# A two-layer attention trunk: buffers, load order and engine for the first unit of value weights

## The chip, the cores and the metric

The kernel runs on one core of a Trainium2 chip. The metric is the device time of one execution in microseconds, median of several. Engines are named as in the profile: PE is TensorE (matmuls), PEld its loading of the stationary operand, DVE VectorE, ACT ScalarE, POOL GpSimd, and SP the engine whose queue issues the DMA transfers.

## The reference

The trunk has two layers. Each takes the RMS norm of the running state h, runs a token mixer with a gate, projects the result and adds its norm to h. Layer 0 mixes by dilated window attention in three groups of 16 heads, layer 1 by differential attention. x has 1024 tokens of 1024 channels, all in float32.

```python
for i in range(DEPTH):                      # 2
    u = rmsnorm(h, norm_pre[i])
    y = dilated_mixer(u, ...) if i % 2 == 0 else diff_mixer(u, ...)
    h = h + rmsnorm(y, norm_post[i])

def dilated_mixer(h, w_in, w_out):
    proj = h @ w_in                         # q, k, v of 3 x 16 heads, and the gate
    ...                                     # v: 3 x 1024 columns
    y = o.reshape(B, S, DIL_WIDTH) * jax.nn.silu(gate)
    return y @ w_out
```

What this case is about is the very first part: the norm of x, its transposition, and the first 512 of the 3072 value columns of layer 0.

## The kernel before, in words

A float32 matmul is done as three matmuls with operands split in a high and a low part: `high` is a cast to a reduced type, `low` is what the cast left out (full minus high). So each weight piece passes three steps: a load into a tile `raw`, a cast on ScalarE into the high tile (`split`, L184), and a subtraction into the low tile (`low`, L122), on the engine that is handed in. The split state of x, transposed, stays in two large tiles, `XH` and `XL`.

The value columns of layer 0 come in six units (`values0(g, u)`), each 1024 x 512 weights. `v_weights` brings a unit in four pieces of 128 x 1024 floats (512 KB): two make one pair of tiles `vwh`, `vwl`, of which three pairs exist. Piece by piece, its tile `raw` comes from `raw_tile`, a ring of two buffers shared by all weights of the kernel. Then, for each of eight blocks of 128 tokens, `v_block` gives 24 matmuls (L213: eight k tiles, and for each high x high, high x low, low x high); the result is copied and split into `vs` (L513 on ScalarE, L122 on VectorE) and stored to DRAM (L515).

The first unit is woven into the start: blocks of x are loaded (L522), normed (`normed`: square and sum on ScalarE, a power on GpSimd, L135, one multiplication on VectorE, L144, that yields `xn`), and transposed on TensorE in eight small matmuls (`to_xt`, L153); ScalarE copies the result to XH (L158), VectorE writes XL. After the transposes of a block come the 24 matmuls of that block, then the next block. The generator of the unit is advanced twice behind the load of block 0 of x, which writes the loading and splitting of its four pieces at that place of the program. The start pool lies on the right side of the on-chip memory and is closed after the first unit.

The order on TensorE is the order of the program. On the other engines, SP's queue among them, a scheduler orders the instructions when the kernel is built: in the order of the program as far as their inputs and buffers are there by its estimated times; otherwise a later instruction goes ahead. A queue then runs strictly in that order, and each instruction waits on the chip for what it needs. The second unit (`values0(0, 1)`) follows in the program after the start.

Of the kernel before, what the change touches and what calls it, by code (L numbers as in the profile page):

```python
# [10 lines left out]
F32 = mybir.dt.float32  # L11
# [7 lines left out]
P = 128  # L19
T = 1024  # L20
D = 1024
# [71 lines left out]
def trunk(ctx: ExitStack, tc: tile.TileContext, a: dict, out: bass.AP):  # L93
    nc = tc.nc
# [26 lines left out]
    def low(eng, o, full, hi):  # L121
        eng.tensor_tensor(o, full, hi.bitcast(F32), ALU.subtract)  # L122
# [15 lines left out]
    def normed(pool, rows, g_b, bufs=None):  # L138

        ss = pool.tile([P, 1], F32, tag="ss", name="ss")  # L140
        xn = pool.tile([P, D], F32, tag="xn", name="xn", bufs=bufs)
        nc.scalar.activation(xn, rows, AF.Square, accum_out=ss)
        r = rstd(pool, ss, 1.0 / D, "pre")
        nc.vector.scalar_tensor_tensor(xn, rows, r, g_b, ALU.mult, ALU.mult)  # L144
        return xn

    def to_xt(xn, n, tag):

        for c in range(2):
            pt = ps.tile([P, 512], F32, tag=tag, name="pt_x")  # L150
            for j in range(4):
                kt = 4 * c + j
                nc.tensor.transpose(  # L153
                    out=pt[:, ts(j)], in_=xn[:, ts(kt)], identity=ident
                )
            src = pt.rearrange("p (j q) -> p j q", j=4)
            hi = XH[:, 4 * c : 4 * c + 4, ts(n)]
            nc.scalar.copy(hi, src)  # L158
            low(nc.vector, XL[:, 4 * c : 4 * c + 4, ts(n)], src, hi)
# [5 lines left out]
    def ts(j, w=P):  # L165
        return slice(j * w, (j + 1) * w)

    def bcast_row(pool, src, tag):
        t = pool.tile([P, D], F32, tag=tag, name=tag, bufs=1)
        nc.sync.dma_start(t, src.partition_broadcast(P))  # L170
        return t


    def raw_tile(shape):
        return wp.tile(shape, F32, tag="raw", name="raw", bufs=2)
# [7 lines left out]
    def split(wh, wl, raw, eng=None):  # L183
        nc.scalar.copy(wh, raw)  # L184
        low(eng or alt(), wl, raw, wh)

    def load(w, shape):
        raw = raw_tile(shape)
        nc.sync.dma_start(raw, w)
        return raw  # L190


    def v_weights(pool, tags, w, n, step, eng):

        parts = []
        for c in range(0, KT, 4):
            wh, wl = (pool.tile([P, 4, n], F32R, tag=t, name=t) for t in tags)
            for k in range(0, 4, step):
                split(wh[:, k : k + step], wl[:, k : k + step],
                      load(w[:, c + k : c + k + step, :], [P, step, n]), eng)  # L200
            parts.append((wh, wl))
            yield 0
        yield parts

    def v_block(parts, n, b, o, first, last):

        k = 0
        for c in range(2):
            for j in range(4):
                wh, wl = (t[:, j, :] for t in parts[c])  # L210
                xh, xl = (t[:, 4 * c + j, ts(b)] for t in (XH, XL))
                for l, r_ in ((xh, wh), (xh, wl), (xl, wh)):
                    nc.tensor.matmul(o, lhsT=l, rhs=r_, start=first and k == 0,  # L213
                                     stop=last and k == 3 * KT - 1, skip_group_check=True)
                    k += 1
                    yield n
# [3 lines left out]
    def qk_unit(pool, unit, w, sub=1, on_pool=False):  # L220

        tiles = []
        for half in range(2):
            wh, wl = w_tiles([P, KT, P])
            split(wh, wl, load(w[half], [P, KT, P]))
            tiles.append((wh, wl))
# [51 lines left out]
    def gate_units(pool, layer, w, fs, eng=None, prepare=None):  # L278

        for f in fs:  # L280
            wh, wl = w_tiles([P, KT, P])
            split(wh, wl, load(w[f], [P, KT, P]), eng)
            if prepare and f == fs[-1]:
                prepare()
                banks = [ps.tile([P, 512], F32, tag="pj", name="pg") for _ in range(2)]
                for k0 in (0, EARLY):
                    for c in range(2):
                        yield from project(banks[c], wh, wl, ts(c, 512), range(k0, k0 + EARLY))
                for c in range(2):
                    yield f, c, banks[c]  # L290
                return
            for c in range(2):
                o = ps.tile([P, 512], F32, tag="pj", name="pg")
                yield from project(o, wh, wl, ts(c, 512))
                yield f, c, o

    def gates(pool, layer, w, fs):

        for v in gate_units(pool, layer, w, fs, nc.vector):
            if type(v) is tuple:  # L300
                f, c, o = v
                s = pool.tile([P, 512], F32, tag="sil", name="sil", bufs=2)
                nc.scalar.activation(s, o, AF.Silu)
                nc.sync.dma_start(sil_d[layer][f, :, ts(c, 512)], s)
                written.add(("gate", layer, f))
            else:
                yield v
# [15 lines left out]
    def run(gen):  # L323
        for _ in gen:
            pass
# [175 lines left out]

    with tc.tile_pool(name="v0", bufs=3) as vp:

        def values0(g, u, eng=nc.vector):
            for parts in v_weights(vp, ("vwh", "vwl"), a["dil_v"][g, u], 512, 2, eng):
                if parts == 0:
                    yield 0
            for b in range(NB):
                pv = ps.tile([P, 512], F32, tag="pj", name="pv")
                yield from v_block(parts, 512, b, pv, True, True)  # L510
                vs = vp.tile([P, 8, 2, HD], F32R, tag="v", name="vs")
                src = pv.rearrange("p (h f) -> p h f", h=8)
                nc.scalar.copy(vs[:, :, 0, :], src)  # L513
                low(nc.vector, vs[:, :, 1, :], src, vs[:, :, 0, :])
                nc.sync.dma_start(  # L515
                    v0_d[g, ts(b), 8 * u : 8 * u + 8, :], vs.rearrange("p h e f -> p h (e f)").bitcast(F32))

        with tc.tile_pool(name="start", bufs=2, side="right") as sp:
            blocks, g_b, v = [], None, values0(0, 0, nc.gpsimd)
            for n in range(NB):  # L520
                xb = sp.tile([P, D], F32, tag="xb", name="xb", bufs=6)
                nc.sync.dma_start(xb, x_v[n])  # L522
                blocks.append(xb)
                if n == 0:
                    g_b = bcast_row(sp, a["norm_pre"][0], "g_b")
                    next(v)
                    next(v)
            for n in range(NB):
                to_xt(normed(sp, blocks[n], g_b), n, "pt")
                for _ in range(24):  # L530
                    next(v)
            run(v)
        run(values0(0, 1))
        run(gates(vp, 0, a["dil_g"], range(8 - LATE0)))
        for g in (1, 2):
            for u in range(2):
                run(values0(g, u))
# [11 lines left out]
    with tc.tile_pool(name="l0", bufs=2) as lp:  # L549
# [216 lines left out]
        for i in range(nst + LAG_P):  # L766
            if i < nst:
                hd, c = heads[i // 4], i % 4
# [16 lines left out]
            if 0 <= i - LAG_T < nst:  # L785
                hd, c = heads[(i - LAG_T) // 4], (i - LAG_T) % 4
# [4 lines left out]
            if 0 <= i - LAG_P < nst:  # L791
                hd, c = heads[(i - LAG_P) // 4], (i - LAG_P) % 4
# [7 lines left out]
    with tc.tile_pool(name="o0", bufs=2, reuse_waits="tile") as op:  # L800
# [10 lines left out]
        def values1(pool, v2, **kw):  # L811

            for parts in v_weights(wp, ("wh", "wl"), a["diff_v"][v2], 256, 4, nc.vector):
                if parts == 0:
                    yield 0
            for b2 in range(NB // 2):
                pv = ps.tile([P, 512], F32, tag="pj", name="pv")


                for e in range(2):  # L820
                    yield from v_block(parts, 256, 2 * b2 + e, pv[:, ts(e, 256)], e == 0, e == 1)
                vs = pool.tile([P, 2, 2, 2, P], F32R, name="vs", **kw)
                src = pv.rearrange("p (b h f) -> p (b h) f", b=2, h=2)
                hi = vs.rearrange("p b h e f -> p (b h) e f")
                nc.scalar.copy(hi[:, :, 0, :], src)
                low(nc.vector, hi[:, :, 1, :], src, hi[:, :, 0, :])
                for e in range(2):
                    nc.sync.dma_start(
                        v1_d[2 * v2 : 2 * v2 + 2, 2 * b2 + e].rearrange("h k c -> k h c"),
                        vs[:, e].rearrange("p h e f -> p h (e f)").bitcast(F32),  # L830
                    )
            written.add(("v", v2))


        v = values1(op, 0, tag="pq")
# [43 lines left out]
    with tc.tile_pool(name="l1", bufs=2) as lp:  # L879
# [163 lines left out]
        for hd in heads:  # L1043
# [7 lines left out]
            for c in range(4):  # L1051
                start, n = h + LAG + c * (c + 1) / 20, c + 1
# [50 lines left out]
```

## Time and profile before

| | |
|---|---|
| time, median of 3 runs | 2029.63 us (2026.72 to 2030.63) |
| the profiled execution | 2031.38 us, its span 2029.5 us |
| mean granted TensorE clock | 0.981 |
| busy: PE, PEld, DVE, ACT, POOL | 94%, 79%, 56%, 44%, 30% of the span |
| DMA | 397.90 MB, mean 196 GB/s |

Times in the profile are microseconds from the start of the span. A row of the timeline gives the start, the duration, the engine, the line of the kernel and what is written from what; in square brackets is how long the engine stood idle before, and who released it. A row of the chain gives start, duration and the engine or transfer that the chain passes through. A row by stretches gives the stretch, its length and the busy time (with the count of instructions) of PE, PEld, DVE, ACT and POOL, then the granted clock of TensorE, the busy share of the DMA engines and GB/s.

### The profile page before, as it was taken

Reading aid. Unit: us, or ns where it says so; the run is one execution under the profiler, and the core shown is the slowest. Engines: PE = TensorE matmul, PEld = TensorE weight load, DVE = VectorE, ACT = ScalarE, POOL = GpSimd, SP = SyncE. Lnnn points to the kernel's source line nnn. Section 1 sums busy time; section 2 is a strip of 40 time slices with the busy share of each in tenths; the row PEclk is TensorE's granted clock in tenths of the full one; section 3 lists DMA queues with packets and bytes.
Section 4 is the critical chain, followed back from the end, with each engine's and each line's share of the span. In section 5 each row is a group of like instructions: output and inputs, shape, how many; then the busy total and the mean of one; then the engine's idle time right before and its main releaser. Section 6 shows DMA issues by size and latency. Waiting matters only on the chain.

```text
span 2029.5 us, 28888 instructions
## 1 busy us (share of the span) xinstructions
PE 1905.9 (94%) x10008; PEld 1594.5 (79%) x10008; DVE 1143.0 (56%) x2771; ACT 888.0 (44%) x2057; POOL 618.0 (30%) x386
## 2 busy tenths in 40 slices
PE   6999999999999998989898978899999999999898
PEld 4788888888878787878787867788878788887776
DVE  3312122146676768676768674571057877878626
ACT  3312122125555555555555565352244445545632
POOL 2000000043353535353535340040471533524111
PEclk8999999999999999999999989999999999999999
DMA  5424244377696969697878889553356555555753
GB/s 208 146 88 140 87 156 152 113 221 229 191 300 195 291 202 293 195 282 218 267 234 240 256 284 294 162 176 107 129 174 193 175 176 164 169 196 182 274 160 125
DMA packets 218018, 397.90 MB, mean 196 GB/s; under 512 B 40976, under 2 KB 123408, under 8 KB 217872
## 3 DMA queue, kind: packets, MB, share of 16 engines
q1 hardware_dynamic: 217872, 396.04, 61.3%
q8 instruction: 80, 1.31, 0.3%
q14 instruction: 66, 0.54, 0.1%
HBM read 254.87 MB, written 132.71 MB: 191 GB/s over the span
## 4 chain that ended last, share of the span: by engine, by line
PE 62%; DMA 13%; DVE 12%; ACT 4%; POOL 4%; issue 3%; SPq 1%; POOLq 0%; DVEq 0%; ACTq 0%
PE pqk L274 22%; PE pv L213 16%; PE pg L274 8%; PE po L386 4%; PE sc L921 2%; PE pe L439 2%; PE up L646 2%; PE sc L596 2%; DMA wb<-wt_d 2%; PE ob L974 2%; DMA st_d<-st 2%; PE tp L619 2%; DVE u L669 1%; POOL r L252 1%; DVE pm L924 1%
## 5 line engine op out<-in xcount | busy, mean ns | idle before, releaser
L274 PE MATMUL pqk<-XL,wh 128*128 128x512 f32 x1024 | 421.1, 411 | 0.0
L274 PE MATMUL pqk<-XH,wh 128*128 128x512 f32 x1024 | 409.3, 400 | 1.7 <-DVE t L251 1.7
L274 PE MATMUL pqk<-XH,wl 128*128 128x512 f32 x1024 | 410.5, 401 | 0.0
L606 ACT ACTIVATE pm<-pm,st 128x128 f32<-128x128 f32 (+1 forms) x384 | 170.2, 444 | 159.7 <-DVE st L603 158.1
L122 POOL TENSOR_TENSOR wl<-raw,wh 128x1024 fp32r<-128x1024 f32 x35 | 84.0, 2400 | 500.6 <-ACT wh L184 500.6
L274 PEld LDWEIGHTS pqk<-XH,wh 128*128 128x128 f32 x1024 | 194.3, 190 | 30.6 <-DVE t L251 2.4
L274 PEld LDWEIGHTS pqk<-XL,wh 128*128 128x128 f32 x1024 | 194.4, 190 | 27.5
L274 PEld LDWEIGHTS pqk<-XH,wl 128*128 128x128 f32 x1024 | 194.8, 190 | 27.0
L250 POOL TENSOR_TENSOR r<-t 128x512 f32<-128x512 f32 x64 | 98.2, 1535 | 266.7 <-DVE t L249 265.7
L122 DVE TENSOR_TENSOR wl<-raw,wh 128x1024 fp32r<-128x1024 f32 x61 | 82.0, 1345 | 149.1 <-ACT wh L184 148.6
L213 PE MATMUL pv<-vwh,XH 128*128 128x512 f32 x384 | 155.8, 406 | 7.0 <-ACT XH L158 4.0
L184 ACT CAST wh<-raw 128x1024 fp32r<-128x1024 f32 x96 | 100.5, 1047 | 140.3 <-PE pqk L274 61.8
L213 PE MATMUL pv<-vwl,XH 128*128 128x512 f32 x384 | 154.9, 403 | 2.8 <-POOL vwl L122 2.8
L213 PE MATMUL pv<-vwh,XL 128*128 128x512 f32 x384 | 154.8, 403 | 0.9 <-DVE XL L122 0.3
L122 DVE TENSOR_TENSOR vs<-pv,vs 128x512 fp32r<-128x512 f32 x64 | 44.2, 691 | 197.3 <-ACT vs L513 191.3
L931 ACT ACTIVATE pm<-pm,mx 128x256 f32<-128x256 f32 (+7 forms) x128 | 99.4, 776 | 120.3 <-DVE mx L930 61.8
L122 DVE TENSOR_TENSOR pp<-tp,pp 128x512 fp32r<-128x512 f32 (+2 forms) x192 | 104.0, 542 | 73.6 <-ACT pp L623 72.0
L619 PE MATMUL tp<-ident,pm 128*128 128x128 f32 x560 | 95.7, 279 | 39.2 <-DVE pp L122 38.2
L603 DVE CUSTOM_DVE_ANT_0 pm<-sc,masks 128x128 f32<-128x128 f32 (+1 forms) x384 | 118.8, 344 | 20.8 <-PE sc L596 19.4
L619 PEld LDWEIGHTS tp<-ident,pm 128*128 128x128 f32 x560 | 72.6, 143 | 73.5 <-issue 34.2
L924 DVE CUSTOM_DVE_ANT_0 pm<-sc,md 128x512 f32<-128x512 f32 (+3 forms) x192 | 102.5, 551 | 32.9 <-PE sc L921 30.1
L513 ACT CAST vs<-pv 128x512 fp32r<-128x512 f32 x48 | 28.2, 587 | 189.9 <-PE pv L213 188.7
(514 smaller groups left out, 4483.6 us busy)
## 6 DMA issues: line engine op xcount, KB each, us to landing
qk_d<-rh SPq DMA_DIRECT2D x64, 512.0 KB
qk_d<-r SPq DMA_DIRECT2D x64, 512.0 KB
qh<-qk_d SPq DMA_DIRECT2D x128, 256.0 KB
ql<-qk_d SPq DMA_DIRECT2D x128, 256.0 KB
ka<-qk_d SPq DMA_DIRECT2D x64, 512.0 KB
v_d<-vs SPq DMA_DIRECT2D x48, 512.0 KB
raw<-in_dil_qk_dram SPq DMA_DIRECT2D x48, 512.0 KB
vt<-v_d SPq DMA_DIRECT2D x48, 512.0 KB
```

The source lines that it names most:

```text
L122: eng.tensor_tensor(o, full, hi.bitcast(F32), ALU.subtract)
L184: nc.scalar.copy(wh, raw)
L213: nc.tensor.matmul(o, lhsT=l, rhs=r_, start=first and k == 0, stop=last and k == 3 * KT - 1, skip_group_check=True)
L250: nc.gpsimd.tensor_sub(put(r[0]), nat(t1), nat(t2))
L274: nc.tensor.matmul(o, lhsT=l[:, kt, :], rhs=r_[:, kt, tok], start=kt == 0 and k == 0, stop=kt == KT - 1 and k == 2)
L386: nc.tensor.matmul(banks[c], lhsT=l[:, kt, ts(n)], rhs=r_[:, ts(c, 512)], start=first and k == 0, stop=last and k == 2,)
L439: nc.tensor.matmul(bank, lhsT=l[:, kt, ts(n)], rhs=r_[:, ts(c, 512)], start=kt == 0 and k == 0, stop=kt == EARLY - 1 and k == 2)
L603: nc.vector.tensor_tensor_reduce(pm[:, cols], sc[:, cols], m[:, m.shape[1] - w_ :], 1.0, 3.0e38, ALU.add, ALU.min, st[:, 0, j : j + 1])
L606: nc.scalar.activation(pm[:, cols], pm[:, cols], AF.Exp, bias=st[:, 0, j : j + 1], scale=-1.0, accum_out=st[:, 1, j : j + 1])
L619: nc.tensor.transpose(out=tp[:, ts(n)], in_=self.pb.pop((b, kb)), identity=ident)
L924: nc.vector.tensor_tensor_reduce(pm[:, k0:k1], sc[:, :w_], m_, 1.0, 3.0e38, ALU.add, ALU.min, mx[:, j : j + 1])
L931: nc.scalar.activation(pm[:, :wq], pm[:, :wq], AF.Exp, bias=mx[:, 0:1], scale=-1.0, accum_out=den)
```

## The change

The four pieces of the first unit no longer use the shared ring of two raw buffers but a ring of four in the start pool; the ring of x's blocks in the same pool goes from six buffers to four. The order of the program stays, but with a buffer free for each piece, no load of the unit has to wait for a buffer. The subtractions of the first unit go from GpSimd to VectorE, where those of the other units are. The shared ring of two is not used by the first unit any more.

```diff
-    def load(w, shape):
-        raw = raw_tile(shape)
+    def load(w, shape, raw=None):
+        raw = raw or raw_tile(shape)
         nc.sync.dma_start(raw, w)
         return raw
...
-    def v_weights(pool, tags, w, n, step, eng):
+    def v_weights(pool, tags, w, n, step, eng, raw=lambda: None):
...
                 split(wh[:, k : k + step], wl[:, k : k + step],
-                      load(w[:, c + k : c + k + step, :], [P, step, n]), eng)
+                      load(w[:, c + k : c + k + step, :], [P, step, n], raw()), eng)
...
-        def values0(g, u, eng=nc.vector):
-            for parts in v_weights(vp, ("vwh", "vwl"), a["dil_v"][g, u], 512, 2, eng):
+        def values0(g, u, **kw):
+            for parts in v_weights(vp, ("vwh", "vwl"), a["dil_v"][g, u], 512, 2, nc.vector, **kw):
...
-            blocks, g_b, v = [], None, values0(0, 0, nc.gpsimd)
+
+            blocks, g_b = [], None
+            v = values0(0, 0, raw=lambda: sp.tile([P, 2, 512], F32, tag="raw", name="raw", bufs=4))
             for n in range(NB):
-                xb = sp.tile([P, D], F32, tag="xb", name="xb", bufs=6)
+                xb = sp.tile([P, D], F32, tag="xb", name="xb", bufs=4)
```

## The prediction

> **What bounds the kernel now.** I read the page first, then the chain that ended last, cut to the first 35 us, then the timeline of SP's queue and of TensorE there, then busy time by stretches.
>
> ```profile
> span 2029.5 us, 28888 instructions
> PE 1905.9 (94%) x10008; PEld 1594.5 (79%) x10008; DVE 1143.0 (56%) x2771; ACT 888.0 (44%) x2057; POOL 618.0 (30%) x386
> 90.00:500.00 410.00, 410.00 (x1837) 332.79 (x1836) 110.79 (x184) 99.97 (x174) 46.54 (x25) 1.00 0.44 148
> 500.00:700.00 200.00, 188.05 (x1039) 158.83 (x1038) 144.10 (x377) 107.89 (x305) 86.05 (x49) 0.98 0.80 239
> ```
>
> The first figures of a stretch are its length and the busy time of PE; the last three are granted clock, DMA share and GB/s. PE is busy 94% of the span and without a gap from 90 to 500 us, so a microsecond by which its stream reaches 90 us earlier is carried on for at least 410 us; later there are gaps (12 us in 200). What the change touches lies ahead of 90 us. The chain there:
>
> ```profile
> 2.13 6.63 DMA raw<-in_dil_v_dram
> ...
> 8.78 1.05 ACT vwh L184
> ...
> 12.29 6.73 DMA raw<-in_dil_v_dram
> ...
> 19.05 1.05 ACT vwh L184
> ...
> 22.49 2.37 POOL vwl L122
> ...
> 24.88 3.60 DMA raw<-in_dil_v_dram
> ...
> 29.58 1.23 DVE vwl L122
> 30.81 0.60 DVE vs L122
> 31.41 0.61 DVE XL L122
> ...
> 32.06 7.77 PE pv L213 x22
> ```
>
> Until 32 us the chain is weights: a load, its cast on ScalarE, its subtraction on GpSimd, which frees the buffer for the next load; from then on it is matmuls. SP's queue says why the third load goes out only at 12.29:
>
> ```profile
> 2.13 0.91 SPq L189 DMA_DIRECT2D raw<-in_dil_v_dram  x2
> 3.08 2.90 SPq L522 DMA_DIRECT2D xb<-in_x_dram  x5
> 8.85 0.33 SPq L522 DMA_DIRECT2D xb<-in_x_dram  x1
> 12.29 2.66 SPq L189 DMA_DIRECT2D raw<-in_dil_v_dram  x2
> 16.49 0.33 SPq L522 DMA_DIRECT2D xb<-in_x_dram  x1
> ...
> 31.43 39.64 SPq L515 DMA_DIRECT2D v_d<-vs  x6
> ```
>
> There are two raw buffers, so pieces 2 and 3 of the first unit wait for GpSimd, and six blocks of x have gone ahead of them. On TensorE (start, length, idle before):
>
> ```profile
> 10.37 0.79 PE L213 MATMUL pv<-vwh,XH 128*128 128x512 f32 x1
> 12.32 0.80 PE L213 MATMUL pv<-vwl,XH 128*128 128x512 f32 x1 [1.16 <-POOL vwl L122]
> 16.76 0.42 PE L213 MATMUL pv<-vwh,XL 128*128 128x512 f32 x1
> 20.15 0.76 PE L213 MATMUL pv<-vwh,XH 128*128 128x512 f32 x1 [2.97 <-ACT vwh L184]
> 22.58 0.79 PE L213 MATMUL pv<-vwl,XH 128*128 128x512 f32 x1 [1.67 <-POOL vwl L122]
> 27.27 1.04 PE L153 MATMUL pt_x<-ident,xn 128*128 128x128 f32 x8
> 32.06 0.79 PE L213 MATMUL pv<-vwh,XL 128*128 128x512 f32 x1 [0.27 <-DVE XL L122]
> 37.32 0.40 PE L213 MATMUL pv<-vwh,XL 128*128 128x512 f32 x1
> 39.65 1.04 PE L153 MATMUL pt_x<-ident,xn 128*128 128x128 f32 x8
> 41.82 0.50 PE L213 MATMUL pv<-vwh,XL 128*128 128x512 f32 x1
> 47.05 1.04 PE L153 MATMUL pt_x<-ident,xn 128*128 128x128 f32 x8
> 26.00:27.00 1.00, 1.00 (x3) 0.72 (x3) 0.00 (x0) 0.99 (x1) 0.00 (x0) 0.50 0.52 184
> 27.00:27.50 0.50, 0.50 (x5) 0.39 (x4) 0.48 (x1) 0.00 (x0) 0.00 (x0) 0.96 0.98 393
> 34.00:37.00 3.00, 3.00 (x9) 2.32 (x8) 0.67 (x1) 0.00 (x0) 0.00 (x0) 0.50 0.46 183
> ```
>
> Block 0 has 24 matmuls, from 10.37 to the transposes at 27.27. It loses 1.16 + 2.97 + 1.67 = 5.80 us waiting for weights, and all of it runs slow: from 32.06 to 37.32 there are 12 steps of 0.43 to 0.44 us from one matmul to the next, with a granted clock of 0.50 in the rows of 34 to 37 and 26 to 27, and block 0 has the same step (eleven matmuls from 12.32 to 16.76; I take 0.425); from 41.82 to 47.05 there are 22 of 0.238 us. So block 1 (27.27 to 39.65, 12.38 us) is dear too: block 2 takes 7.40.
>
> **The change part by part.** *Buffers and loads.* The four pieces of the first unit get four buffers of their own in the start pool; x's fall from six to four. With no wait left, the four loads stand in program order behind the first x block and the row of norm weights, and ahead of x's blocks 1 to 3. The two shared raw buffers are free from the start, so the second unit's first two pieces can go out next, while block 4 waits for block 0 to be normalised. When does each land? From the row of this stretch a 512 KB load takes 524288 B / 413 GB/s = 1.27 us; SP's issues (0.33 to 0.48 each) are faster.
>
> ```profile
> 11.00:20.00 9.00, 5.01 (x12) 3.44 (x11) 3.58 (x7) 3.81 (x7) 4.62 (x4) 1.00 1.03 413
> 10.21 1.05 ACT L184 CAST vwh<-raw 128x1024 fp32r<-128x1024 f32 x1
> L122 POOL TENSOR_TENSOR vwl<-raw,vwh 128x1024 fp32r<-128x1024 f32 x4 | 9.4, 2363 | 7.8 <-ACT vwh L184 7.8
> L122 DVE TENSOR_TENSOR vwl<-raw,vwh 128x1024 fp32r<-128x1024 f32 x2 | 2.5, 1226 | 10.7 <-ACT vwh L184 10.7
> L144 DVE SCALAR_TENSOR_TENSOR xn<-xb,r,g_b 128x1024 f32<-128x1024 f32 x3 | 3.8, 1283 | 2.2 <-DMA g_b<-in_norm_pre_dram 1.1 <-POOL r L135 1.1
> L122 DVE TENSOR_TENSOR XL<-pt_x,XH 128x512 fp32r<-128x512 f32 x2 | 1.4, 692 | 2.6 <-ACT XH L158 2.6
> ```
>
> Piece 1 is there by 10.2 (its cast). As a test, piece 2 now comes seven loads later: 10.2 + 7 x 1.27 = 19.1, and its cast starts at 19.05. Changed: piece 2 at 11.5, 3 at 12.8, x 1 to 3 at 14.0, 15.3, 16.6, the second unit's pieces at 17.8 and 19.1. Casts take 1.05 us, so pieces 2 and 3 are cast by about 13.9, after the two of block 0's XH.
>
> *Subtractions.* Four leave GpSimd (2.36 us each) for VectorE (1.23). VectorE then has, between 7.2 and 20 us: block 0's normalising 1.28, four subtractions 4.9, two XL 1.38, blocks 1 and 2 normalised 2.57: 10.1 of 12.8 us, so it fits, but nearly full. Piece 0: cast until 9.84, subtracted by 11.1, XL behind it by 11.8, piece 1 by 13.0, the second XL 13.7, pieces 2 and 3 by 14.9 and 16.1, block 1 normalised by 17.6. GpSimd keeps only the small power, which comes sooner; nothing waits for it longer.
>
> *Block 0.* The first matmul stays at 10.37, the second moves from 12.32 to 11.1, the third starts at 11.8, and then none waits: at 0.425 us piece 1 is wanted at 13.1, piece 2 at 15.6, piece 3 at 18.2 (12 and 18 matmuls in), all there but for a tenth or so. At that pace the 24th starts at 11.8 + 21 x 0.425 = 20.7.
>
> *The clock.* It rises in the rows after a busy stretch: at 27.0 after 4.4 us (from 22.58; after the gap at 27.27 to 32.06 it is slow again), and at 37.32 after 5.26 us (from 32.06) or 6.75 with the two matmuls ahead of that. For the changed start 11.8 + 5.26 = 17.1, which I take since it is the rise that lasted; the ends are 16.2 and 18.5. By 17.1 15 matmuls have started; the other nine take 0.238 each, and the transposes start at 19.4 (ends: 19.0 and 20.0). That is 27.27 - 19.4 = 7.9 us earlier.
> [...]
>
> *Block 1.* The steady block takes 7.40 us, of which 2.17 (39.65 to 41.82) lie between transposes and third matmul. Now that gap is 4.79 (27.27 to 32.06), as the second unit's subtraction (29.58 in the chain) stands ahead of block 1's XL on VectorE: 2.62 more. After the change those pieces land at 17.8 and 19.1: cast until 20.1, subtracted until 21.4, then the copy's remainder 0.60 and XL 0.61, third matmul at 22.6 instead of 21.6. So 1.0 us stays (0 to 2.62). Block 1 ends at 19.4 + 7.4 + 1.0 = 27.8, against 39.65.
>
> *Blocks 2 to 7 and after.* x's blocks 4 to 7 now go out when blocks 0 to 3 have been normalised, four blocks ahead of their use, 30 us for a load of 3.6 us (24.88 to 28.48): nothing. POOL and DMA work later is the same. The order on every engine but TensorE comes from a scheduler that works on estimated times; shifting the start can rearrange later queues. No row prices that; bounded by the gaps, 12 us in 200 from 500 on, I take nothing and let it widen the chances on both sides.
>
> Sum: 39.65 - 27.8 = 11.8 us. The profiled execution took 2031.38, so 2019.6; the median, 1.75 lower, would give 2017.8; I take the middle, **2018.7**. With the ends of clock and block 1 the gain is 9.6 to 13.3: the case's own range is 2016.3 to 2021.8.
>
> **The rivals.** *The clock stays slow through block 0*, since VectorE is nearly full and its order leaves small waits. Transposes at 21.2, block 1 as in the trace less its 2.62 plus 1.0 (10.8): 32.0, gain 7.7, 2022 to 2024. For it: 12.32 to 16.76 brought no faster step.
>
> *The change doesn't do what it says*: the scheduler still puts x's three blocks ahead of pieces 2 and 3. Piece 2 at 15.3, cast 16.4, subtracted 17.6, where 16.0 is wanted: 1.6 us lost and the rise of the clock delayed, gain 8 to 9, 2021.5. Against: only the missing buffer put them behind.
>
> *Given back later.* The stretches after 500 us have gaps that PE's stream waits in; if an order changes there for the worse by 8 us or more, the total stays within 0.2% (4 us, about what a measurement here can tell from no change), near 2029; by 16 it is slower, near 2036. For it: PE is idle 124 us in all (2029.5 - 1905.9). Against: 90 to 500 is gapless, so queues behind it see the same distances.
>
> *Slower: x's late blocks.* With four buffers a load of x stands on SP behind stores of values, each of which waits for a block's end. If block n+4's load came behind block n+3's store, each of blocks 4 to 7 would wait 3.6 us for the load and 1.3 for its normalising, and up to 4.2 from block's end to store (27.27 to 31.43): 4.9 to 9.1 us, 28 in all at the middle, so 2018.7 + 28 = 2047. One store earlier 7.4 of each are covered and at most 1.7 left, so that place decides. Against: the last x load (16.49) stands ahead of the first store (31.43), and then waited for block 1's normalising alone.
>
> **How the numbers follow.** Forecast 0.55; clock 0.15; order of loads 0.08; given back to no change 0.12, beyond it 0.05; x's blocks 0.05. Faster 0.78, same 0.12, slower 0.10. The range goes from 2016.3 less the spread of the runs below their median (2.9) to 2023.7 plus as much, **2013.5 to 2027**.
>
> **What would show it.** SP: four raw loads in a row ahead of x's block 1. TensorE: no wait for weights between 12 and 19 us, transposes of block 1 near 19.4 instead of 27.27, steps of 0.238 from about 17, transposes of block 2 near 27.8, and blocks of 7.4 us from there. The prediction is wrong if the loads are in another order, if VectorE's XL waits behind subtractions, or if the stretches after 500 us have more gaps than now.

## The result, and the profile after

The changed kernel takes 2019.11 us (median of 6 runs, 2013.53 to 2023.45); the kernel before took 2032.03 us in the 6 runs counted with them. The ratio is 0.9937, with a 95% interval of 0.9916 to 0.9958: 8.5 to 17 us less. The profiled execution took 2018.35 us, with a span of 2016.5 us, 13.0 less than that of before.

SP's queue in the timeline of the changed kernel (start, duration, what is issued):

```profile
2.13 1.97 SPq L189 DMA_DIRECT2D raw<-in_dil_v_dram  x4
4.14 1.73 SPq L524 DMA_DIRECT2D xb<-in_x_dram  x3
7.17 1.91 SPq L189 DMA_DIRECT2D raw<-in_dil_v_dram  x2
11.42 6.67 SPq L524 DMA_DIRECT2D xb<-in_x_dram  x2
70.53 1.46 SPq L189 DMA_DIRECT2D raw<-in_dil_g_dram  x2
```

Four pieces in a row stand ahead of x's blocks 1 to 3, and the second unit's first two behind them. The last row is used below as a mark: the first load of gate weights can only go out when a shared raw buffer is free, and that hangs on the end of the first unit (the second unit's last two pieces hold both buffers until the first unit's weight tiles are free). In the kernel before, the same row is

```profile
83.76 1.46 SPq L189 DMA_DIRECT2D raw<-in_dil_g_dram  x2
```

so the mark came 13.23 us sooner and the span became 13.0 shorter. The start of the changed kernel by the timeline of TensorE, VectorE and ScalarE:

```profile
9.84 1.23 DVE L122 TENSOR_TENSOR vwl<-raw,vwh 128x1024 fp32r<-128x1024 f32 x1 [1.26 <-ACT vwh L184]
11.70 2.00 ACT L184 CAST vwh<-raw 128x1024 fp32r<-128x1024 f32 x2
11.72 0.79 PE L213 MATMUL pv<-vwh,XL 128*128 128x512 f32 x1
13.17 0.63 PE L213 MATMUL pv<-vwh,XL 128*128 128x512 f32 x1
13.32 2.35 DVE L122 TENSOR_TENSOR vwl<-raw,vwh 128x1024 fp32r<-128x1024 f32 x2
13.59 0.53 PE L213 MATMUL pv<-vwh,XH 128*128 128x512 f32 x1
13.96 0.39 PE L213 MATMUL pv<-vwl,XH 128*128 128x512 f32 x1
14.19 0.39 PE L213 MATMUL pv<-vwh,XL 128*128 128x512 f32 x1
16.39 1.29 DVE L144 SCALAR_TENSOR_TENSOR xn<-xb,r,g_b 128x1024 f32<-128x1024 f32 x1 [0.66 <-POOL r L135]
17.91 1.04 PE L153 MATMUL pt_x<-ident,xn 128*128 128x128 f32 x8
19.34 1.28 DVE L144 SCALAR_TENSOR_TENSOR xn<-xb,r,g_b 128x1024 f32<-128x1024 f32 x1
20.53 0.68 DVE L122 TENSOR_TENSOR XL<-pt_x,XH 128x512 fp32r<-128x512 f32 x1
21.13 1.22 DVE L122 TENSOR_TENSOR vwl<-raw,vwh 128x1024 fp32r<-128x1024 f32 x1
21.27 0.50 PE L213 MATMUL pv<-vwh,XL 128*128 128x512 f32 x1 [1.29 <-DVE XL L122]
26.48 1.04 PE L153 MATMUL pt_x<-ident,xn 128*128 128x128 f32 x8
33.88 1.04 PE L153 MATMUL pt_x<-ident,xn 128*128 128x128 f32 x8
```

What to see: the waits for weights are gone; the step from one matmul to the next falls from 0.42 us (13.17 to 13.59) to 0.23 (13.96 to 14.19); transposes of block 1 start at 17.91 instead of 27.27, of block 2 at 26.48 instead of 39.65, and then blocks take 7.40 as before. On VectorE, block 2's norm (19.34) stands ahead of block 1's XL (20.53), and the second unit's subtraction (21.13) behind it.

Busy time from 7 to 20 us, before and after (length, then PE, PEld, VectorE, ScalarE, GpSimd):

```profile
7.00:20.00 13.00, 7.51 (x20) 5.30 (x20) 5.52 (x8) 6.03 (x9) 5.71 (x4) 1.00 1.03 413
```

```profile
7.00:20.00 13.00, 11.05 (x42) 8.17 (x42) 9.80 (x12) 9.13 (x13) 1.09 (x2) 1.00 1.02 401
```

The DMA engines are full in both; what came through was in another order, and TensorE did 42 instructions in the time of 20. The granted clock of these rows reads 1.00 in both, although steps of 0.42 to 0.43 us lie in them: in both traces the record of the clock begins with its first rise (16.80 before, 13.87 after). At the start it is the step that has to be read.

### The profile page after: what moved, and what is told of

It reads as the page before. It is cut to its first block, busy times and chain, and to the rows that moved or that the text cites. A ratio compares the mean times of both kernels' runs of the same rounds, so it can differ in the third digit from the quotient of the medians.

```text
span 2016.5 us, 28889 instructions
## 1 busy us (share of the span) xinstructions
PE 1904.8 (94%) x10008; PEld 1596.0 (79%) x10008; DVE 1146.4 (57%) x2775; ACT 887.4 (44%) x2057; POOL 608.3 (30%) x382
## 4 chain that ended last, share of the span: by engine, by line
PE 70%; DVE 10%; DMA 10%; ACT 3%; issue 3%; POOL 3%; SPq 1%; POOLq 0%; DVEq 0%; ACTq 0%
PE pqk L274 26%; PE pv L213 16%; PE pg L274 8%; PE po L386 4%; PE pe L439 3%; PE sc L598 3%; PE sc L923 3%; PE up L648 2%; DMA wb<-wt_d 2%; PE tp L621 2%; PE ob L976 2%; DMA qh<-qk_d 1%; DVE u L671 1%; DMA st_d<-st 1%; PE tp L956 1%
```

## The experiments

The theory: the gain is what TensorE no longer loses ahead of the mark (waits, and the slow clock that they bring), and it is carried to the end. Rivals: the one or the other part of the change brings it alone; the clock alone brings it; later waits give it back. Each kernel's mark and transposes are read from its profile, since they repeat to some tenths of a microsecond (the mark is at 83.76 and 84.05 in two profiles of the kernel before, at 70.53 and 70.52 in two of the change), where totals scatter by several (2013.53 to 2023.45 for the change).

**The loads alone: subtractions of the first unit back on GpSimd.**

```diff
-            v = values0(0, 0, raw=lambda: ...bufs=4))
+            v = values0(0, 0, nc.gpsimd, raw=lambda: ...bufs=4))
```

`values0` takes the engine as an argument again.

> The first unit's four pieces have buffers of their own, as in the change, but are subtracted on GpSimd, as before. Theory (the loads are most of it, the engine paces block 0): pieces cast by 13.9 us, four subtractions of 2.36 us in a row on GpSimd end near 12.2, 14.6, 17.0 and 19.4, so the last six matmuls wait for the fourth; transposes of block 1 near 20.7 us (17.9 in the change, 27.3 before), of block 2 near 29.3 (26.5; 39.65), the span 2.8 us over the changed kernel's, 2019.3, ratio to before 0.995. Rival (the engine is as important as the loads): GpSimd falls behind, its power for block 1's norm stands behind all four subtractions, transposes of block 1 after 22.5 us and half or less of the 13 us left, span 2023 or more.

Measured: ratio 0.9976 (0.9964 to 0.9989). Rows of its timeline:

```profile
9.40 9.40 POOL L122 TENSOR_TENSOR vwl<-raw,vwh 128x1024 fp32r<-128x1024 f32 x4 [2.56 <-ACT vwh L184]
18.73 1.08 POOL L135 TENSOR_TENSOR r<-v,half_neg 128x1 f32<-128x1 f32 x2
20.77 1.07 PE L153 MATMUL pt_x<-ident,xn 128*128 128x128 f32 x8 [0.48 <-DVE xn L144]
25.41 0.80 PE L213 MATMUL pv<-vwh,XL 128*128 128x512 f32 x1 [2.59 <-DVE XL L122]
32.02 1.03 PE L153 MATMUL pt_x<-ident,xn 128*128 128x128 f32 x8
76.09 1.46 SPq L189 DMA_DIRECT2D raw<-in_dil_g_dram  x2
```

Block 1's transposes came when expected (20.77 against 20.7), but not for the expected reason alone: they waited 0.48 us for block 1's norm, whose power stands behind all four subtractions on GpSimd (18.73), as the rival had it. Block 1 was dearer than expected: the norms of blocks 1 and 2 pile up on VectorE with the second unit's subtractions, XL is late, and TensorE's pause of 2.59 us costs the clock (0.43 us steps until 28.1). The mark is 7.7 us sooner than before's instead of 13.2, still more than the half or less of the rival. So with the loads in place the engine is worth 5.6 us, twice what was expected; half of that comes in block 1, through the norms queued behind the subtractions.

**The engine alone: VectorE, but shared buffers and the old loads.**

```diff
-            blocks, g_b, v = [], None, values0(0, 0, nc.gpsimd)
+            blocks, g_b, v = [], None, values0(0, 0)
```

> The subtractions of the first unit go to VectorE, but buffers and loads are as before (two shared raw buffers, six for x). Theory (the loads' place in the queue bounds block 0): piece 2 may be issued about 1.2 us sooner, but lands near 19 us all the same, since six blocks of x stand ahead; its subtraction ends near 21.3 instead of 22.5; transposes of block 1 near 26.1, of block 2 near 37, the span 2 to 3 us under before's, about 2027, ratio 0.9987. Rival (the engine is as important): 6 us or more are gained, transposes of block 2 at 33.5 or sooner.

Measured: ratio 0.9996 (0.9980 to 1.0011); transposes of block 1 at 25.96 and of block 2 at 36.23, the mark at 80.30, 3.5 us sooner. Piece 2 was cast at 19.27, as late as before:

```profile
15.45 0.33 SPq L522 DMA_DIRECT2D xb<-in_x_dram  x1
19.27 1.05 ACT L184 CAST vwh<-raw 128x1024 fp32r<-128x1024 f32 x1 [5.46 <-DMA raw<-in_dil_v_dram]
20.37 0.79 PE L213 MATMUL pv<-vwh,XH 128*128 128x512 f32 x1 [4.55 <-ACT vwh L184]
```

The theory holds: a sooner issue behind six blocks of x buys nothing. The two parts give 7.7 and 3.5 us alone and 13.2 together.

**Own buffers and VectorE, but pieces 2 and 3 behind x's blocks 1 to 3.**

```diff
                 if n == 0:
                     g_b = bcast_row(sp, a["norm_pre"][0], "g_b")
                     next(v)
+                if n == 3:
                     next(v)
```

> As the change, but pieces 2 and 3 stand behind the loads of x's blocks 1 to 3 in the program, so only the order of the loads differs. Theory (a place in the queue is worth its landing time): pieces 2 and 3 land near 15.3 and 16.6 us, piece 2 is subtracted by 17.6, where the matmuls of the changed kernel wanted it from 15.1; transposes of block 1 near 20.1 us instead of 17.9, span 2.2 us over the changed kernel's, about 2018.7; if the gap of 2.3 us costs the clock, up to 5 us more. Rival (with buffers of their own the order is without weight): no difference to the change, transposes of block 1 at 17.9 and span 2016.5.

Measured: ratio 0.9947 (0.9924 to 0.9970); the mark at 75.12, 4.6 us later than the change's.

```profile
15.40 1.05 ACT L184 CAST vwh<-raw 128x1024 fp32r<-128x1024 f32 x1 [1.33 <-DMA raw<-in_dil_v_dram]
16.04 1.29 DVE L144 SCALAR_TENSOR_TENSOR xn<-xb,r,g_b 128x1024 f32<-128x1024 f32 x1 [0.43 <-POOL r L135]
16.50 0.50 PE L213 MATMUL pv<-vwh,XH 128*128 128x512 f32 x1 [0.84 <-ACT vwh L184]
18.52 0.79 PE L213 MATMUL pv<-vwl,XH 128*128 128x512 f32 x1 [1.52 <-DVE vwl L122]
19.11 0.63 PE L213 MATMUL pv<-vwh,XL 128*128 128x512 f32 x1
23.37 1.69 PE L153 MATMUL pt_x<-ident,xn 128*128 128x128 f32 x8
```

Piece 2 was cast at 15.40, as worked out. The edit moves the casts and subtractions of pieces 2 and 3 behind as well, so that block 2's norm (16.04) stands ahead of piece 2's subtraction on VectorE. TensorE's two pauses of 0.84 and 1.52 us brought the clock down, so that the last 11 matmuls ran at 0.43 us, and transposes of block 1 started at 23.37 instead of 17.91, 3.3 later than expected. Of these 5.46 us, 2.8 are lost over the two pauses, 2.3 to the slow steps behind them, and 0.4 ahead of them; block 1 gives 0.9 back, as its XL is in time. So the order counts, and about as much through the clock as through the wait.

**The kernel before with the clock up: extra matmuls on a constant tile in its waits.**

```diff
+            fill0 = {1: 3, 12: 18, 13: 8}
+            spin(16)
             for n in range(NB):
                 to_xt(normed(sp, blocks[n], g_b), n, "pt")
+                if n == 1:
+                    spin(14)
-                for _ in range(24):
+                for i in range(24):
                     next(v)
+                    if n == 0 and i + 1 in fill0:
+                        spin(fill0[i + 1])
```

`spin(n)` issues n matmuls of 128 x 512 whose result nobody reads.

> The kernel before, with extra matmuls on a constant tile (results unused) in front of block 0 and in its waits for weights, sized to fit in them, so that the clock is up all through. Theory (waits and clock are worth less one by one than together): block 0 still waits until 20.15 and 22.58 for its pieces, the other matmuls take 0.238 us, transposes of block 1 near 25.2 us; block 1 still waits for the second unit's subtraction until 32.06, then runs at 0.238: transposes of block 2 near 37.3 instead of 39.65, span about 2.4 us less, 2027.2, ratio 0.9988. Rival (the clock is half of the gain by itself): 38 slow matmuls at 0.19 us each are gained, 7.2 us: transposes of block 2 near 32.4, span 2022.

Measured: ratio 0.9999 (0.9985 to 1.0013); transposes of block 1 at 26.35, of block 2 at 36.01, the mark at 80.12, 3.6 us sooner. The extra matmuls from 16.90 to 21.0 filled the wait, and those behind it ran at 0.23 us, but the waits stayed: the last piece was still waited for until 25.07. The clock was not up all through. In this kernel both casts of the first two pieces stand ahead of XH on ScalarE, the first matmul waited 2.17 us for it, and the steps were 0.43 us from 13.4 until 15.5. What the extra matmuls bring is 3.6 us at the mark, not the 7.2 of the rival, and not by the clock alone: block 1's XL also went ahead of the second unit's later subtraction. The price of the clock by itself stays open.

**The change once more, as a mark for the next three.** 

> The changed kernel once more, on the chip of the next three, as their mark. Theory (a microsecond won ahead of the second unit is carried to the end): first load of gate weights near 70.5 us of the span, time from there to the end as long as that of the other kernels on this chip to within 2 us, ratio to before 0.9937 within its interval of 0.9916 to 0.9958. Rival (a part of the gain hung on the one chip): ratio above 0.9958.

Measured: ratio 0.9934 (0.9912 to 0.9956), the mark at 70.52, from there to the end of the span 1950.2 us, 4.2 longer than in the first profile. The gain stood. That the rest takes the same time to within 2 us in all kernels on this chip did not come true: it took 1950.2 us here and 1948.5, 1954.9 and 1944.3 in the profiles of the next three (clock up, delayed, transposes ahead). The stretch after the mark will be looked at below.

**The change with the clock up at its start.**

```diff
+            spin(16)
             for n in range(NB):
```

> The change, with 16 extra matmuls on a constant tile (results unused) ahead of the first transposes, so that the clock is up when block 0 starts. Theory (with the weights there, block 1's norm on VectorE ends late enough to bind): block 0's matmuls run at 0.238 us from the start and end near 16.9, but block 1 is normalised near 17.6 as in the change, so its transposes start near 17.7 instead of 17.9, and the gain is under 0.5 us, ratio to the change 0.9998. Rival (what is left of slow clock is still paid): eight slow matmuls at 0.19 us, 1.5 us sooner, transposes of block 1 near 16.4 to 16.9.

Measured: ratio 0.9943 (0.9922 to 0.9965), the mark at 70.92, 0.4 later. Both were wrong:

```profile
9.75 1.05 ACT L184 CAST vwh<-raw 128x1024 fp32r<-128x1024 f32 x1 [0.25 <-DMA raw<-in_dil_v_dram]
10.71 1.07 ACT L158 CAST XH<-pt_x 128x512 fp32r<-128x512 f32 x2
11.34 0.50 PE L213 MATMUL pv<-vwh,XH 128*128 128x512 f32 x1 [1.76 <-ACT XH L158]
12.71 0.50 PE L213 MATMUL pv<-vwh,XL 128*128 128x512 f32 x1 [0.64 <-DVE XL L122]
13.28 0.40 PE L213 MATMUL pv<-vwl,XH 128*128 128x512 f32 x1
13.51 0.52 PE L213 MATMUL pv<-vwh,XL 128*128 128x512 f32 x1
13.83 0.63 PE L213 MATMUL pv<-vwh,XH 128*128 128x512 f32 x1
14.26 0.63 PE L213 MATMUL pv<-vwl,XH 128*128 128x512 f32 x1
19.48 1.03 PE L153 MATMUL pt_x<-ident,xn 128*128 128x128 f32 x8
```

The clock was up at the start (0.23 us steps to 13.5), and was lost there, behind pauses of 1.76 and 0.64 us, until about 17. Block 0's transposes took 1.09 instead of 1.97 us, but block 0 ended 1.6 us later. The pauses come from another order of instructions: here ScalarE casts the second piece (9.75) ahead of XH (10.71; in the change 9.79), and VectorE does both subtractions ahead of XL. So the run does not show what a fast clock alone would bring to the change; it shows that extra matmuls ahead of such pauses bring nothing. The mark is only 0.4 later since block 1 took 7.38 instead of 8.57 us.

**The change with TensorE delayed.**

```diff
+            spin(16 + 56)
             for n in range(NB):
```

> The change, with 72 extra matmuls on a constant tile (results unused) ahead of the first transposes: TensorE reaches block 0 about 11.7 us later, near 20.3 us, with the clock up and all its operands there. Theory (the delay goes to the end undiminished): block 1's transposes near 27.7, block 2's near 35.8 instead of 26.5, first load of gate weights near 79.8, the total 9.3 us over the change's, and the time from that load to the end unchanged. Rival (what is late at the start is made up in the later waits): the total less than 5 us over the change's.

Measured: ratio 0.9986 (0.9976 to 0.9997), against 0.9934 of the change beside it: medians 2032.84 and 2022.19, 10.7 us apart. The mark came at 78.37, 7.85 later. The total is over the change's by at least what the mark is late; nothing was made up, and the rival (under 5 us) falls. Block 1's transposes came at 26.95, 0.75 sooner than expected, and block 1 took 7.38 us, without the extra of the change, since its operands had long been there.

**Later steps: x's buffers, and the order on VectorE.** One buffer for x's blocks (`bufs=1` for `xb`):

> The change, with one buffer for x's blocks instead of four, so that each block's load waits for the norm of the one before and stands behind the second unit's pieces. Theory (only block 1 has no lead to lose): block 1's x lands near 20.4 us, its transposes start near 23.8 instead of 17.9, the clock falls in that gap for 2 to 3 us more, later blocks take their 7.4 us since load, square, power and norm (about 6.5 us in all) fit into a block; first load of gate weights at 77 to 80 us instead of 70.5, total 7 to 9 us over the change's, ratio to before 0.998. Rival (x's late blocks each wait for their load, 5 to 9 us a block, the prediction's slower case): first load of gate weights at 95 us or later, ratio above 1.005.

Measured: ratio 0.9984 (0.9970 to 0.9997), the mark at 80.36, 9.8 later than the change's. Transposes came at 21.48, 30.45, 43.71, 51.09: those of block 1 late as expected, but by less; block 2 took 13.26 us, 5.9 more than a steady block, which was not expected; then 7.38 a block.

```profile
32.84 1.06 ACT L142 ACTIVATE xn<-xb 128x1024 f32<-128x1024 f32 x1 [5.95 <-DMA xb<-in_x_dram]
33.90 0.57 ACT L513 CAST vs<-pv 128x512 fp32r<-128x512 f32 x1
34.36 1.08 ACT L158 CAST XH<-pt_x 128x512 fp32r<-128x512 f32 x2
```

The square of block 3 waits for its x, and block 1's copy and block 2's XH, long due (transposes at 30.45), stand behind it on ScalarE. So even with one buffer, late loads cost once, not at every block; the prediction's slower case is not near. With four, no block of x was waited for after block 2.

One buffer for the normed block (`normed(sp, blocks[n], g_b, bufs=1)`):

> The change, with one buffer instead of two for the normed block xn, so that block 2 can be normed only after block 1's transposes have read theirs; on VectorE block 2's norm then comes after block 1's XL and the second unit's first subtraction stays behind XL as it is. Theory (in the changed kernel it is block 2's norm, 19.34 to 20.62, that stands ahead of block 1's XL, not the second unit's subtraction): the third matmul of block 1 follows its transposes by 2.2 to 2.4 us instead of 3.36, transposes of block 2 near 25.4 instead of 26.5, steady blocks still 7.4, total 1.1 us less, which the ratio won't show (0.9932 against 0.9937). Rival (the second unit's subtraction is the cause, as the prediction had it): the gap stays at 3 us or more.

Measured: ratio 0.9933 (0.9908 to 0.9958); the mark at 68.96, 1.6 sooner.

```profile
17.60 1.06 PE L153 MATMUL pt_x<-ident,xn 128*128 128x128 f32 x8
19.70 0.51 PE L213 MATMUL pv<-vwh,XL 128*128 128x512 f32 x1
18.97 0.68 DVE L122 TENSOR_TENSOR XL<-pt_x,XH 128x512 fp32r<-128x512 f32 x1
19.83 1.23 DVE L122 TENSOR_TENSOR vwl<-raw,vwh 128x1024 fp32r<-128x1024 f32 x1 [0.19 <-ACT vwh L184]
24.93 1.03 PE L153 MATMUL pt_x<-ident,xn 128*128 128x128 f32 x8
```

The gap from transposes to third matmul is 2.10 us instead of 3.36, with the second unit's subtraction where it was. So in the changed kernel it was block 2's norm that held block 1's XL.

**Transposes ahead by half a block**, a further change of order, in two versions; the second adds `bufs=1` to both calls of `normed`:

```diff
+            to_xt(normed(sp, blocks[0], g_b), 0, "pt")
             for n in range(NB):
-                to_xt(normed(sp, blocks[n], g_b), n, "pt")
-                for _ in range(24):
+                for i in range(24):
                     next(v)
+                    if n + 1 < NB and i + 1 == (12 if n else 24):
+                        to_xt(normed(sp, blocks[n + 1], g_b), n + 1, "pt")
```

> The change, with the transposes of block n+1 put behind the twelfth of block n's 24 matmuls from block 1 on (block 1's own stay behind block 0), so that casts and subtractions of XH and XL run beside matmuls. Theory (each steady block of 7.40 us holds 24 matmuls of 0.234, the transposes of 1.04 and 0.7 us of waits for XH and XL): blocks of 6.7 us, six of them, 4.4 us in all, first load of gate weights near 66.1 us instead of 70.5, total 4.4 us less than the change's. Rival (the split of values or the norms then bind on VectorE): blocks stay at 7.2 us or more, under 1.5 us.

Measured: mark at 64.03, 6.5 sooner than the change's, with blocks of 6.44 us (transposes 22.82, 29.26, 35.71) instead of the 6.7 expected. Median 2018.32 against 2022.19 of the change beside it, ratio 0.9912 (0.9884 to 0.9940) against 0.9934: the intervals overlap, so that it beats the change is likely by the mark, and not shown by the totals.

> The transposes ahead by half a block, as in the run before, and one buffer for the normed block: both savings together. Theory (they add): first load of gate weights near 62.9 us (64.0 with the transposes ahead alone, 70.5 in the change), total 7.6 us under the change's, ratio to before 0.990. Rival (with one buffer the norm of the next block comes too late for transposes half a block ahead): blocks above 6.6 us, first load of gate weights at 65 or later.

Measured: mark at 66.23, ratio 0.9927 (0.9909 to 0.9944).

```profile
24.94 1.06 PE L153 MATMUL pt_x<-ident,xn 128*128 128x128 f32 x8 [2.65 <-DVE xn L144]
```

The rival holds in part: block 2's transposes wait 2.65 us for their norm, once, and the mark is behind 65; but the later blocks take 6.46 us, not above 6.6. The two savings don't add.

**The kernel before once more.** The spans of the later profiles are longer behind the mark than those of the first two.

> The kernel before once more, with a profile, since the spans of the single changes and of the change on later chips end 1948 to 1955 us after the first load of gate weights, against 1945.7 (before) and 1946.0 (change) in the first two profiles. Theory (that part is the run's, not the kernel's): first load of gate weights at 83.8 us as before, and from there 1948 to 1955 us here too, span 2032 to 2039. Rival (the single changes give 3 to 6 us back later): 1946 again, span 2029.5.

Measured: 2039.99 us in this one execution (another of the same kernel beside it took 2031.37), span 2038.1, mark at 84.05, and so 1954.1 us behind it against 1945.7 in the first profile of the same kernel, as the theory had it. Busy time in the stretch from 1000 to 1200 us behind the mark, in the first profile of before, then here:

```profile
1083.76:1283.76 200.00, 178.61 (x951) 148.38 (x949) 130.23 (x342) 111.78 (x306) 62.45 (x34) 0.94 0.86 268
```

```profile
1083.76:1283.76 200.00, 173.44 (x930) 145.04 (x929) 128.52 (x341) 113.07 (x308) 66.09 (x36) 0.93 0.88 268
```

That TensorE is 5 us less busy in this stretch is the run's doing, not the kernel's. So the profiles of the two single changes (marks 76.09 and 80.30, ends 1952.2 and 1951.5 later) don't show that these give something back. The median span of all runs of a kernel, less its mark (83.9 for the kernel before), tells more. The change has 1949.9 us behind the mark on the chip of its second profile, and the kernel before, on the same chip, 1950.2: the change gives back nothing that can be seen. In the same way the loads alone and the engine alone have 1952.0 and 1952.1, and the kernel before with extra matmuls 1953.3, against 1950.6 of the kernel before on their chip. Whether they give back one to three microseconds, or this is scatter, is not shown; by its total the run with the loads alone gains 4.9 us (2.2 to 7.3), where its mark says 7.7. Why a run loses 5 us in that stretch stays open.

## Why the prediction was right, point by point

It said 2018.7, in 2013.5 to 2027, with 11.8 us gained; 2019.11 was measured, and 13.2 us at the mark. That the time came within 0.4 us is luck in part: the gain was 1.4 us too small, and the runs of the kernel before that were counted with the change have a median of 2032.03, 2.4 above the one that the prediction started from.

- *Order and landing of the loads*: as worked out. Pieces 2 and 3 were cast by 13.70 (said: 13.9). The run with late loads shows that this order, of the loads and of the splits behind them, carries 4.6 us, and the first two runs that neither part does it alone.
- *Subtractions on VectorE*: the chain ended at 15.67 (16.1), block 1's norm at 17.68 (17.6), the third matmul came at 11.72 (11.8). That VectorE "fits, but nearly full" was right: it was busy 9.80 of 13 us, and block 1's norm ended only 0.23 us ahead of its transposes. That the power on GpSimd comes sooner was said, but given no worth; by the trace of the run with the loads alone, the power behind four subtractions is a good part of the 5.6 us that the engine is worth there.
- *The clock*: the term that was mis-sized. It took 17.1 for the rise (16.2 to 18.5), counted as 5.26 us from the third matmul; steps of 0.23 began about 13.9. The transposes came at 17.91 instead of 19.4, outside the ends of 19.0 to 20.0. It counted from too late: TensorE is busy without a gap from its first transposes at 8.64, and from there the rise took 5.2 us. In five other starts without a gap (the change again, one x buffer, one norm buffer, transposes ahead twice) it came 4.0 to 5.5 us behind the first transposes, between 12.4 and 14.2, much like the 4.4 and 5.26 that the prediction had read; with the engine alone, where TensorE has no gap before 15.8 either, the steps of 0.23 began about 15.1, 6.7 us behind the first transposes at 8.41. In the five but the one with one x buffer, block 1's transposes came between 17.4 and 17.9, with its norm ready 0.1 to 0.4 us before: a still earlier rise would have brought little. That 12.32 to 16.76 of the kernel before "brought no faster step" was misread: the matmul at 16.76 lasts 0.42 us, those before it 0.61 to 0.63, and the record of the clock has its first rise at 16.80 and then a fall at 20.21, in this row:

```profile
20.00:20.50 0.50, 0.35 (x1) 0.26 (x1) 0.00 (x0) 0.32 (x2) 0.33 (x1) 0.71 0.67 270
```

So the clock rose as that stretch ended, and had fallen again by 20.21, at the end of the wait of 2.97 us behind it. What sets the moment of a rise is not shown.

- *Block 1*: right in size and wrong in cause. 1.0 us over the steady gap was forecast, 1.19 measured (3.36 against 2.17), but the second unit's subtraction, which the prediction named, came behind XL; block 2's norm stood ahead of it. The run with one norm buffer shows it, and that the size fits is luck.
- *Carried to the end*: 13.2 at the mark, 13.0 in the span; the delayed run lost in full. The order of instructions on TensorE did not change, and that on the other engines only at the start and between 1230 and 1260 us.
- *Rivals*: the clock did not stay slow, the loads kept their order, nothing that can be seen was given back, and x's blocks were not late. The tested form of the last cost 9.8 us with one buffer, where a loss at each block would have been 28.
- *The range*: its upper end was for a slow clock; the totals of single runs spread by 8 to 10 us, more than the 2.9 that was added.

## What to carry to other kernels

Where a stream of matmuls starts up, count for each operand when it lands in the one queue of transfers, and give the first consumer's weights buffers of their own so that their loads stand ahead of what is wanted later. Waits can cost twice, by themselves and by the clock (with the late loads, 2.8 us over two pauses of 0.84 and 1.52 us, and 2.3 in the slow steps behind them), and two causes of waits were not additive here: 7.7 and 3.5 us alone, 13.2 together. A helper engine that is slow but "off the path" may carry a tiny step of the path in its queue, as the norm's power did behind four subtractions.

## What was not expected of the hardware

With the late loads the clock was lost behind two pauses of 0.84 and 1.52 us within 2.9 us (up to 16.50 and 18.52), with steps of 0.43 us from 19.11 to 23.37; with the clock up, behind pauses of 1.76 and 0.64 us within 3.1 (up to 11.34 and 12.71), with such steps from 13.83 to 16.82. The changed kernel's pauses of 0.29 and 1.29 us (up to 19.23 and 21.27) lost nothing: the steps from 21.60 on are 0.23 to 0.24 us, and the record of its clock reads 1.00 there. A single pause of 2.59 us (the loads alone, up to 25.41) was followed by steps of 0.43 us, and one of 2.65 us (transposes ahead with one norm buffer, up to 24.94) by steps of 0.23 to 0.24. So a sharp limit in the length of a pause is not shown, nor what decides in its place. In the trace of the kernel before, the clock's changes at the start, at 16.80, 20.21, 27.04, 30.45 and 37.28, lie 3.41 or 6.83 us apart.

And the same program, with the same start to 0.3 us, took 1945.7 and 1954.1 us for the rest, in two executions.
